# Filling counts in the last stick-breaking head and in the scan, and a five-step block ranking

## The chip, the cores and the metric

The kernel runs on one core of a Trainium2 chip. TensorE (PE in the profile) multiplies matrices, VectorE (DVE), ScalarE (ACT) and GpSimd (POOL) do elementwise work, SyncE (SP) issues the DMA transfers; each engine takes its own instructions in a fixed order and waits on semaphores for the others. The metric is the device time of one execution in microseconds (us), as a median over runs.

## The reference

One decoder layer on x of 1 x 1024 x 1024 in float32. Three mixers read one projection, each is projected back and merged by sigmoid gates, then come an output projection and a gated feed-forward network:

```python
h = rms_norm(x, pre_mix_norm[l])
proj = h @ w_in[l]
z, xbc, dt_raw, sb_qkv, nsa_q, nsa_kv, nsa_gate, merge_gate = jnp.split(proj, split_points(), axis=-1)
y_ssm = ssm_mixer(z, xbc, dt_raw, ...)
y_sb = stick_breaking_attention(sb_qkv)
y_nsa = nsa_attention(nsa_q, nsa_kv, nsa_gate, ...)
gm = jax.nn.sigmoid(merge_gate.astype(jnp.float32)).reshape(bsz, s, 3, D_MODEL)
mixed = (gm[:, :, 0] * (y_ssm @ w_br_ssm[l]) + gm[:, :, 1] * (y_sb @ w_br_sb[l])
         + gm[:, :, 2] * (y_nsa @ w_br_nsa[l])).astype(x.dtype)
x = x + rms_norm(mixed @ w_out[l], post_mix_norm[l])
```

The sparse attention (NSA) ranks 16 blocks of 64 keys for each query by the probabilities of its compressed attention, and keeps eight; some blocks are forced in and later ones are out:

```python
imp_pad = jnp.pad(p_cmp.sum(axis=2), ((0, 0), (0, 0), (0, 0), (1, 0)))
imp = (imp_pad.reshape(bsz, g, NSA_QBLK, nb, ratio).sum(axis=-1)
       + jnp.pad(imp_pad[..., ratio::ratio], ((0, 0), (0, 0), (0, 0), (0, 1))))
imp = jnp.where(valid, jnp.where(forced, BIG, imp), NEG)
_, idx = lax.top_k(imp, n_sel)
```

Stick-breaking attention (four heads) weighs each key by exp(log sigmoid + a sum over the later keys); the SSD scan runs over eight chunks of 128 positions in four groups of heads.

## The kernel before

Every f32 product of the dense projections is made of three: the high part of the weight by the high and the low part of the data, and the low part of the weight by the high part of the data (hi and lo, whi and wlo in the names). All PE instructions are issued at line 235. The program runs in stages: start and the units of the scan's input until about 305 us, preparation and loop of NSA until 745, the stick-breaking heads until about 1080, the scan until about 1275, and then the branch products' rest, output projection and feed-forward network.

Long chains (a score, its exponentials, its products) would leave PE idle, so each stage draws on a pool of independent dense products, a `Fill`: `take(n)` emits n steps of it. A fine step is three products of 128x512. The gates of the merge (tiles named dense, with h_hi and h_lo) fill the attention stages, the branch projections of the three mixers fill the scan (`branches`). What isn't taken in time is emitted at the stage's end by `rest`.

**Stick-breaking.** `attend` (L1470) runs two chains for each head, for the later and the earlier half of the queries: the first with score tiles in ps_s and output in ps_o, the second with ps_t and ps_b. A chain has three steps for each key block: `score` (three products into a bank, then minimum L1411, exponentials L1412 and L1413, copy L1415, maximum L1416), `carry` (one row subtracted L1426, s_hi L1429 on ACT, s_lo L1430 on POOL, and two products of them into the score's bank) and `value` (sum L1441, exponential L1442, w_hi L1446 on ACT, w_lo L1447 on DVE, three products into the output). After each chain step `attend` adds SB_FILL[h] to a remainder and takes its whole part from the pool. In the last head a second pool, `late`, gives two steps more after each chain step past the 24th, bound behind the third last value product; from chain step 30 on the emission order is kept for PE, and ahead of that a scheduler sets it.

**Ranking.** `compressed` (L1065) handles one tile of 128 queries and one key group. From tile 4 on (eight tiles in all) it ranks: sum over the four heads (L1100), sum over the four compressed positions of a block (L1103), on POOL the next block's first position added (L1105), forced and late blocks set by a factor and a summand from `fa` (L1106, L1107), the eight largest (L1109), those replaced by −3e38 (L1111), a comparison that finds which were not replaced (L1112), and times −1e30 into the bf16 tile `aug` (L1113). PE transposes aug, and L1135 copies it into the rows of Q1 that meet the block rows of `c_aug` in the score product, so that blocks not kept get −1e30.

**Scan.** The loop over n steps four generators, one for each group q; a generator stops at "front" (a chunk's preparation), "heads" and "late" (gating, norm and split of a group's result, which make `E.ys[k, h]`, two for each q and half h). `fronts(0)` and `fronts(1)` step the even and odd groups, and `take(SSD_FILL)` with SSD_FILL = 2 fills behind each. The pool's last products read E.ys through k: output unit 0 first six k, unit 1 four, then the last two k of unit 0 (group 3), then the rest. In the names, even groups' rows are `row` and odd groups' `third`.

## Time and profile before

| what | us |
|---|---|
| median of three runs | 2115.36 (2114.43 to 2115.45) |
| profiled execution, its own time | 2113.84 |
| span of the profiled execution | 2111.9 |
| PE busy | 2081.4 |
| DVE, POOL, ACT busy | 1288.7, 1228.7, 1174.8 |

The mean granted clock of TensorE was 0.999. The span is counted from the first to the last instruction. A row of the timeline has the start in the span, the duration, engine, line, operation, the tile written and those read, the shapes, how many were joined (x3), and in brackets the idle time before it with what ended it. Durations of PE products overlap: how long PE needs for one is read from the distance of two starts.

### The profile page before, as it was taken

To read this page: it belongs to the slowest core of one execution; us is meant where nothing else is said; L and a number is where in the kernel's file an instruction comes from. 1 tells how busy PE (TensorE), PEld (TensorE's weight loads), DVE (VectorE), ACT (ScalarE), POOL (GpSimd) and SP (SyncE) were. 2 spreads that over 40 slices of the span, in tenths; PEclk is the share of its full clock that TensorE was granted. 3 is DMA by queue.
4 is the path that set the end of the run, shared out by engine and by line. 5 is a ranking of instruction groups with operands and counts; after the bars stand their busy time and mean duration, and the time that the engine had idled before them with its cause. 6 is when DMAs were issued, how large, how long until landed. Compare 5 with 4: busy or idle time off the path is not lost.

```text
span 2111.9 us, 29407 instructions
## 1 busy us (share of the span) xinstructions
PE 2081.4 (99%) x10069; PEld 1684.8 (80%) x10069; DVE 1288.7 (61%) x2639; ACT 1174.8 (56%) x2124; POOL 1228.7 (58%) x1223
## 2 busy tenths in 40 slices
PE   9999999999999999999999999999999999999998
PEld 7788888877776778888868878887878888888888
DVE  7854453368477046656557774258866666676765
ACT  6554442367757646667765652246554445576634
POOL 1277763158757633334336875557877777766843
PEclk9999999999999999999999999999999999999999
DMA  7333347321220111223274423444223332265532
GB/s 272 95 116 114 110 148 240 110 90 57 78 75 9 45 48 58 63 70 130 91 256 153 147 68 108 141 150 146 86 77 100 100 104 96 100 214 170 160 118 107
DMA packets 129237, 243.92 MB, mean 115 GB/s; under 512 B 14344, under 2 KB 39592, under 8 KB 129088
## 3 DMA queue, kind: packets, MB, share of 16 engines
q1 hardware_dynamic: 127136, 238.94, 34.5%
q10 hardware_dynamic: 1952, 3.11, 0.4%
q8 instruction: 79, 1.29, 0.3%
q14 instruction: 70, 0.57, 0.1%
HBM read 175.83 MB, written 66.17 MB: 115 GB/s over the span
## 4 chain that ended last, share of the span: by engine, by line
PE 87%; DVE 6%; ACT 3%; POOL 2%; issue 1%; DMA 1%; POOLq 0%; ACTq 0%; DVEq 0%; SPq 0%
PE dense L235 57%; PE ps_s L235 10%; PE ps_o L235 8%; PE ps_t L235 7%; PE psn L235 3%; PE ps_b L235 2%; DVE ps_t L1157 0%; DVE x L1922 0%; ACT x L777 0%; DVE u L356 0%; DMA y<-y_d 0%; ACT wT L1189 0%; DMA q_d<-uhi 0%; POOL wlo L308 0%; DVE x L2123 0%
## 5 line engine op out<-in xcount | busy, mean ns | idle before, releaser
L308 POOL TENSOR_TENSOR wlo<-wraw,whi 128x256 fp32r<-128x256 f32 x300 | 239.8, 832 | 171.6 <-ACT whi L303 166.9
L688 POOL TENSOR_TENSOR ulo<-uf,uhi 128x256 fp32r<-128x256 f32 (+1 forms) x174 | 188.8, 1111 | 147.1 <-ACT uhi L712 96.6
L235 PE MATMUL dense<-h_hi,whi 128*128 128x512 f32 x656 | 260.3, 397 | 0.9 <-ACT gate_e L277 0.9
L235 PE MATMUL dense<-h_lo,whi 128*128 128x512 f32 x656 | 256.6, 391 | 0.0
L235 PE MATMUL dense<-h_hi,wlo 128*128 128x512 f32 x656 | 256.4, 391 | 0.0
L1200 POOL TENSOR_TENSOR wT_lo<-wT,wT_hi 128x512 fp32r<-128x512 f32 x132 | 168.4, 1293 | 54.6 <-ACT wT_hi L1199 50.7
L235 PE MATMUL dense<-x,uhi 128*128 128x512 f32 x600 | 190.6, 389 | 0.0
L235 PE MATMUL dense<-hi,wlo 128*128 128x512 f32 x448 | 176.6, 395 | 0.5 <-POOL wlo L308 0.3
L235 PE MATMUL dense<-hi,whi 128*128 128x512 f32 x448 | 174.4, 390 | 0.0
L235 PE MATMUL dense<-lo,whi 128*128 128x512 f32 x448 | 173.2, 391 | 0.0
L235 PEld LDWEIGHTS dense<-h_hi,wlo 128*128 128x128 f32 x656 | 123.2, 188 | 26.6
L235 PEld LDWEIGHTS dense<-h_hi,whi 128*128 128x128 f32 x656 | 123.4, 188 | 24.2 <-ACT gate_e L277 1.1
L235 PEld LDWEIGHTS dense<-h_lo,whi 128*128 128x128 f32 x656 | 123.5, 188 | 23.2
L303 ACT ACTIVATE whi<-wraw 128x1024 fp32r<-128x1024 f32 x76 | 80.3, 1057 | 96.9 <-PE dense L235 87.5
L235 PEld LDWEIGHTS dense<-x,uhi 128*128 128x128 f32 x600 | 112.6, 188 | 23.7
L688 POOL TENSOR_TENSOR wlo<-wraw,whi 128x256 fp32r<-128x256 f32 (+1 forms) x83 | 94.4, 1164 | 60.8 <-ACT whi L703 60.7
L1430 POOL TENSOR_TENSOR s_lo<-sa,s_hi 128x512 fp32r<-128x512 f32 (+2 forms) x48 | 54.2, 1130 | 129.3 <-ACT s_hi L1429 129.3
L356 DVE SCALAR_TENSOR_TENSOR u<-dense,pv,u 128x511 f32<-128x511 f32 (+1 forms) x140 | 103.4, 741 | 33.2 <-ACT u L352 33.0
L1189 ACT ACTIVATE wT<-ps_s 128x512 f32<-128x512 f32 x132 | 78.2, 595 | 47.8 <-PE ps_s L235 42.4
L235 PE MATMUL dense<-x,ulo 128*128 128x512 f32 x264 | 102.9, 390 | 0.0
L235 PEld LDWEIGHTS dense<-hi,wlo 128*128 128x128 f32 x448 | 84.1, 188 | 20.8 <-issue 1.7
L1157 DVE CUSTOM_DVE_ANT_0 ps_t<-ps_t,edges 128x256 f32<-128x256 f32 (+3 forms) x160 | 82.4, 526 | 28.9 <-PE ps_t L235 27.8
(589 smaller groups left out, 5809.0 us busy)
## 6 DMA issues: line engine op xcount, KB each, us to landing
wraw<-in_wfm SPq DMA_DIRECT2D x62, 512.0 KB, 3.9
wraw<-in_wup SPq DMA_DIRECT2D x48, 512.0 KB, 3.6
lo<-m_d SPq DMA_DIRECT2D x58, 256.0 KB, 2.7
g_d<-gate_e SPq DMA_DIRECT2D x48, 256.0 KB, 3.0
s_d<-o SPq DMA_DIRECT2D x48, 256.0 KB, 2.0
m_d<-u SPq DMA_DIRECT2D x44, 256.0 KB, 2.0
row<-g_d SPq DMA_DIRECT2D x36, 256.0 KB, 2.7
row<-s_d SPq DMA_DIRECT2D x32, 256.0 KB, 4.1
```

Of the source, the lines that this page charges most:

```text
L235: return pin(f(*a, **k), in_order)
L303: act(hi, raw, AF.Copy)
L308: eng.tensor_tensor(lo[:, s], raw[:, s], fl(hi[:, s]), op=OP.subtract)
L356: V.scalar_tensor_tensor(o[:, d:], ps[:, :512 - d], taps[d], o[:, d:], op0=OP.mult, op1=OP.add)
L688: eng.tensor_tensor(lo[:, s], x[:, s], fl(hi[:, s]), op=OP.subtract)
L1157: V.tensor_tensor_reduce(pm[:, :w], pm[:, :w], edges[:, 0:w] if edge else edges[:, 640 - w:], 1.0, -3e38, op0=OP.add, op1=OP.max, accum_ou ...
L1189: act(w.rearrange("p h q -> p (h q)"), pz, AF.Exp)
L1200: P.tensor_tensor(lo, wf, fl(hi), op=OP.subtract)
L1430: (P if SB_SLO else V).tensor_tensor(s_lo[:, c0:], a[:, c0:], fl(s_hi[:, c0:]), op=OP.subtract)
```

## The change

It has three parts. In the last stick-breaking head the filling is 1.9 steps behind each chain step instead of 2. In the ranking the sum over heads goes into a tile `sums` that holds for each block four positions and a fifth value, the forced or late summand, which the DMA brings with it; one reduction over six neighbours (four positions, the summand, the next block's first position) gives the ranked value, match_replace writes −1e38 straight into aug, and the copy into Q1 becomes the comparison "greater than −1e37", against block rows of `c_aug` that now hold −1e30. In the scan, four steps in place of two are taken where the first pair of groups has started (n is 1) and behind a "late" stage of groups 2 and 3 in `fronts(1)`.

```diff
-        aug[0, b, b * 64:(b + 1) * 64] = 1.0
+        aug[0, b, b * 64:(b + 1) * 64] = NEG
...
-    fa = np.stack([fac, add], 1).reshape(8, 128, 32).transpose(1, 0, 2).reshape(128, 256)
+    fa = np.zeros((128, 4, 17, 5), f)
+    fa[:, :, :16, 4] = add.reshape(8, 128, 16)[4:].transpose(1, 0, 2)
+    fa = fa.reshape(128, 340)
...
-SB_FILL = (2.2, 2.2, 2.2, 2)
+SB_FILL = (2.2, 2.2, 2.2, 1.9)
...
-    fa = kp.tile([128, 8, 2, 16], F32, name="fa")
-    nc.sync.dma_start(fa.rearrange("p a b c -> p (a b c)"), A["c_fa"])
+    sums = kp.tile([128, 4, 85], F32, name="sums")
+    nc.sync.dma_start(sums.rearrange("p i n -> p (i n)"), A["c_fa"])
...
-            imp = wk.tile([128, 64], F32, name="imp")
-            V.tensor_reduce(imp, p.rearrange("p h n -> p n h"), axis=AX, op=OP.add)
+            s = sums[:, i - 4]
+            blocks = s[:, :80].rearrange("p (b r) -> p b r", r=5)[:, :, 0:4]
+            V.tensor_reduce(blocks, p.rearrange("p h (b r) -> p b r h", r=4), axis=AX, op=OP.add)
             im = wk.tile([128, 16], F32, name="im")
-            iv = imp.rearrange("p (b r) -> p b r", r=4)
-            V.tensor_reduce(im, iv, axis=AX, op=OP.add)
-
-            P.tensor_tensor(im[:, 0:15], im[:, 0:15], iv[:, 1:16, 0], op=OP.add)
-            P.tensor_tensor(im, im, fa[:, i, 0, :], op=OP.mult)
-            P.tensor_tensor(im, im, fa[:, i, 1, :], op=OP.add)
+            six = s[:, 0:81]
+            six = bass.AP(tensor=six.tensor, offset=six.offset, ap=[six.ap[0], [5, 16], [1, 6]])
+            V.tensor_reduce(im, six, axis=AX, op=OP.add)
             top = wk.tile([128, 8], F32, name="top")
             V.max(top, im)
-            left = wk.tile([128, 16], F32, name="left")
-            V.match_replace(left, in_to_replace=top, in_values=im, imm_value=-3e38)
-            V.tensor_tensor(left, left, im, op=OP.is_equal)
-            V.tensor_scalar(aug[:, 64:80], left, NEG, None, op0=OP.mult)
+            V.match_replace(aug[:, 64:80], in_to_replace=top, in_values=im, imm_value=-1e38)
...
-            V.tensor_copy(Q1[64:80, :].rearrange("p (h q) -> p h q", h=4),
-                          p2[64:80, None, :128].to_broadcast([16, 4, 128]))
+            V.tensor_scalar(Q1[64:80, :].rearrange("p (h q) -> p h q", h=4),
+                            p2[64:80, None, :128].to_broadcast([16, 4, 128]), -1e37, None, op0=OP.is_gt)
...
-                    filled = q > 1 or stage[q] == "front"
+                    fills = SSD_FILL * (1 if stage[q] == "front" else (1 + part) * (q > 1))
...
-                    if filled:
-                        take(SSD_FILL)
+                    take(fills)
...
-                take(SSD_FILL if n else SSD_AHEAD)
+                take(SSD_FILL * (1 + (n == 1)) if n else SSD_AHEAD)
```

The numbers move instructions. On PE in the last stick-breaking head, before, between the fourth and the third score from the end of the ps_s chain. ps_s_10434 is a score tile (A), ps_s_10499 the next (B); 18 dense products stand between the ps_t score ahead and B's, of which the last three are shown:

```order
L235 MATMUL dense_10568<-h_hi_82,whi_10561 128x512
L235 MATMUL dense_10568<-h_lo_83,whi_10561 128x512
L235 MATMUL dense_10568<-h_hi_82,wlo_10562 128x512
L235 MATMUL ps_s_10499<-row_9387,row_9390 128x512
L235 MATMUL ps_s_10499<-row_9389,row_9390 128x512
L235 MATMUL ps_s_10499<-row_9387,row_9392 128x512
L235 MATMUL ps_s_10434<-s_hi_10452,rtab_74 128x512
L235 MATMUL ps_s_10434<-s_lo_10453,rtab_74 128x512
L235 MATMUL ps_o_10114<-w_hi_10480,row_9395 128x512
L235 MATMUL ps_o_10114<-w_hi_10480,row_9397 128x512
L235 MATMUL ps_o_10114<-w_lo_10481,row_9395 128x512
```

The same place after the change, where A is ps_s_10357 and B ps_s_10428; the ps_t score's last products are the first two rows:

```order
L236 MATMUL ps_t_10511<-row_9332,row_9334 128x512
L236 MATMUL ps_t_10511<-row_9330,row_9336 128x512
L236 MATMUL dense_10447<-h_hi_82,whi_10375 128x512
L236 MATMUL dense_10447<-h_lo_83,whi_10375 128x512
L236 MATMUL dense_10447<-h_hi_82,wlo_10376 128x512
L236 MATMUL ps_s_10428<-row_9331,row_9334 128x512
L236 MATMUL ps_s_10428<-row_9333,row_9334 128x512
L236 MATMUL ps_s_10428<-row_9331,row_9336 128x512
L236 MATMUL ps_s_10357<-s_hi_10390,rtab_74 128x512
L236 MATMUL ps_s_10357<-s_lo_10391,rtab_74 128x512
L236 MATMUL ps_o_10058<-w_hi_10415,row_9339 128x512
L236 MATMUL ps_o_10058<-w_hi_10415,row_9341 128x512
```

Between the ps_t score and B's stand three dense products now, and the dense products that stood there follow P's value products, the last of which comes behind these rows.

On DVE at the same place, before, from A's minimum on (L1441 with ps_s reads the tile ahead of A, P):

```order
L1411 TENSOR_SCALAR sa<-ps_s 128x512
L1416 TENSOR_TENSOR sa<-ps_s,sa 128x512
L1426 TENSOR_TENSOR sa<-sa,ps_s 1x512
L1441 TENSOR_TENSOR sz<-sz,ps_s 128x512
L1411 TENSOR_SCALAR sa<-ps_t 128x512
```

and after (the lines are four lower):

```order
L1407 TENSOR_SCALAR sa<-ps_s 128x512
L1407 TENSOR_SCALAR sa<-ps_t 128x512
L1412 TENSOR_TENSOR sa<-ps_s,sa 128x512
L1422 TENSOR_TENSOR sa<-sa,ps_s 1x512
L1437 TENSOR_TENSOR sz<-sz,ps_s 128x512
L1407 TENSOR_SCALAR sa<-ps_s 128x512
```

The ps_t score's minimum has moved ahead of A's maximum, and so ahead of the reading of P's bank.

On PE in the scan, before, behind the transposes (ps_t<-ident,row) of group 3's first half, from the last transpose of the next chunk's preparation to the products of unit 0 that read group 3's rows (the last two rows):

```order
L235 MATMUL ps_t<-third 128x128
L235 MATMUL ps_s<-row,whi 128x512 x2
L235 MATMUL ps_s<-row,wlo 128x512
L235 MATMUL ps_s<-row,whi 128x512 x2
L235 MATMUL ps_s<-row,wlo 128x512
L235 MATMUL ps_s<-third,whi 128x512 x2
L235 MATMUL ps_s<-third,wlo 128x512
L235 MATMUL ps_s<-third,whi 128x512 x2
L235 MATMUL ps_s<-third,wlo 128x512
L235 MATMUL ps_s<-third,whi 128x512 x2
L235 MATMUL ps_s<-third,wlo 128x512
```

After, from those transposes of group 3's first half on:

```order
L236 MATMUL ps_t<-ident,row 128x128 x4
L236 LDWEIGHTS sel
L236 MATMUL dense<-row,sel 128x512
L236 MATMUL ps_t<-ident,third 128x128 x3
L236 MATMUL ps_t<-third 128x128
L236 MATMUL ps_s<-third,whi 128x512 x2
L236 MATMUL ps_s<-third,wlo 128x512
L236 MATMUL ps_s<-third,whi 128x512 x2
L236 MATMUL ps_s<-third,wlo 128x512
```

The 12 products of the units' earlier rows that stood between are gone from here (they stand ahead of the transposes), and the products that read group 3's rows are the next but the preparation.

## The prediction

> **What bounds the kernel.** I read the busy times and the chain on the page first, then TensorE's list of waits, then the timeline at each place where the change moves something.

> ```profile
> PE 2081.4 (99%) x10069; PEld 1684.8 (80%) x10069; DVE 1288.7 (61%) x2639; ACT 1174.8 (56%) x2124; POOL 1228.7 (58%) x1223
> PEclk9999999999999999999999999999999999999999
> PE 87%; DVE 6%; ACT 3%; POOL 2%; issue 1%; DMA 1%; POOLq 0%; ACTq 0%; DVEq 0%; SPq 0%
> ```

> TensorE is busy for 2081.4 of 2111.9 us, and the chain that ended last is 87% its own. The change removes no matrix product. So nothing is won but TensorE's idle time, 2111.9 − 2081.4 = 30.5 us in the whole program, and nothing is lost but new idle time. VectorE and GpSimd are busy for about 60%; work taken from them counts only where TensorE waits for it. Each term below is therefore a wait of TensorE that goes, or one that comes.

> **Unit of filling.** Neighbouring dense products start 0.23 us apart (1067.46 and 1067.69 in the fence after next; the listed 0.39 overlaps the next product). A step of filling is three, 0.69 us.

> **Part 1, the last stick-breaking head (1.9 steps in place of 2).** The lower count delays filling, and the printed order shows where it goes: the fourth score tile from the end of the ps_s chain (call the last four A, B, C, D) has about as many dense products behind it as before, 150 against 151. Behind B stand 144 against 120, behind C 119 against 84, behind D 84 against 72. So filling that stood between A and B now stands behind B.

> What goes: behind D two places were too thin.

> ```profile
> 1056.95 0.40 PE L235 MATMUL dense<-h_hi,wlo 128*128 128x512 f32 x1
> 1058.37 0.96 PE L235 MATMUL ps_s<-row 128*128 128x512 f32 x3 [1.01 <-DVE sz L1441]
> ```
> ```profile
> 1067.46 0.39 PE L235 MATMUL dense<-h_lo,whi 128*128 128x512 f32 x1
> 1067.69 0.39 PE L235 MATMUL dense<-h_hi,wlo 128*128 128x512 f32 x1
> 1068.67 0.73 PE L235 MATMUL ps_o<-w_hi,row 128*128 128x512 f32 x2 [0.59 <-ACT w_hi L1446]
> 1069.82 0.50 PE L235 MATMUL ps_o<-w_lo,row 128*128 128x512 f32 x1 [0.42 <-DVE w_lo L1447]
> ```

> Start to start, less the products themselves, these cost 1.42 − 0.23 = 1.19, 0.98 − 0.23 = 0.75 and 1.15 − 0.46 = 0.69: **2.6 us**. After, D has 35 instead of 12 dense products ahead of it, and the pair of w_hi 12 instead of 6 (1.4 us more). I take all 2.6 as gone.

> What comes: look at what hung between A and the values of the tile ahead of it (call that tile P).

> ```profile
> 1033.30 0.28 PE L235 MATMUL ps_b<-w_lo,row 128*128 128x256 f32 x1
> 1033.57 0.69 DVE L1411 TENSOR_SCALAR sa<-ps_s 128x512 f32<-128x512 f32 x1 [1.96 <-PE ps_s L235]
> ...
> 1037.02 2.83 POOL L308 TENSOR_TENSOR wlo<-wraw,whi 128x256 fp32r<-128x256 f32 x4 [6.70 <-ACT whi L303]
> ...
> 1037.94 0.62 ACT L1429 ACTIVATE s_hi<-sa 128x512 fp32r<-128x512 f32 x1
> ...
> 1039.81 1.34 POOL L1430 TENSOR_TENSOR s_lo<-sa,s_hi 128x512 fp32r<-128x512 f32 x1
> ...
> 1040.51 0.62 ACT L1446 ACTIVATE w_hi<-sz 128x512 fp32r<-128x512 f32 x1
> ...
> 1041.15 0.69 DVE L1447 TENSOR_TENSOR w_lo<-sz,w_hi 128x512 fp32r<-128x512 f32 x1 [1.16 <-ACT w_hi L1446]
> ...
> 1043.61 0.40 PE L235 MATMUL ps_o<-w_lo,row 128*128 128x512 f32 x1
> 1043.84 0.40 PE L235 MATMUL dense<-h_hi,whi 128*128 128x512 f32 x1
> ```

> A's products are done at 1033.3. Its s_lo exists only at 39.81 + 1.34 = 1041.15, because GpSimd first splits a weight (2.83 us); P's w_lo exists at 41.15 + 0.69 = 1041.84. Before, 31 dense products filled that time, and A's s_hi and s_lo products and P's value products followed at once, until 1043.84. After, only 6 dense products stand there: behind the ps_t score come three, then B's score, A's s_hi and s_lo, and P's three value products, with no dense product between them. TensorE reaches B's score at about 1036.5 (the 1033.3 plus 14 products, the narrow ones shorter). B's bank is that of P, which L1441 frees; in the new order on VectorE L1441 stands behind the ps_t score's L1411. That gives 1038.6. A's s_lo keeps the same two operations ahead of it on GpSimd: about 1041.1. P's w_hi now follows A's s_hi and the ps_t score's exponentials on ScalarE: about 1042.2, w_lo 43.1. So the value products end near 1043.4, 0.44 us earlier than before, with 24 dense products (24 × 0.23 = 5.5 us) still to run. Five us of new idle time: **+5.0**. Bounds: 0 below (if those dense products could run ahead after all; they cannot in this order unless the chain is faster), 5.5 above. The nearest rows are those quoted, so I take 5.0. Queued behind the waiting products are the 24 dense ones and, for those, ScalarE's gates (L277), which nobody needs soon. Part 1: 5.0 − 2.6 = **+2.4 us**.

> Nothing waited for TensorE's filling between 960 and this place, so the slightly thinner filling there costs nothing; its cover is the rest of the filling, and a whole product less at each step would cost 0.23.

> **Part 2, the ranking (eight tiles).** It takes L1105 to L1107 from GpSimd and L1112 and L1113 from VectorE; L1103 reads 96 elements instead of 64.

> ```profile
> L1105 POOL TENSOR_TENSOR im<-im,imp x8: 218/227/235, 448.9 to 652.1; 128x15 f32<-128x15 f32 x8
> ...
> L1109 DVE MAX8 top<-im x8: 172/173/178, 450.3 to 655.2; 128x8 f32<-128x16 f32 x8
>   PEld ps_t L235: 0.5, 1
> L1112 DVE TENSOR_TENSOR left<-left,im x8: 165/354/1207, 450.9 to 656.7; 128x16 f32<-128x16 f32 x8
>   PEld ps_t L235: 0.2, 1
> L1113 DVE TENSOR_SCALAR aug<-left x8: 156/175/690, 451.4 to 657.4; 128x16 bf16<-128x16 f32 x8
> ```

> By the medians that is 8 × (0.35 + 0.18) = 4.2 us off VectorE and 8 × 3 × 0.22 = 5.4 off GpSimd. L1135 becomes a comparison of the same 16x512 tile from PSUM, L1111 writes bf16: both at the old price. The wider L1103 and the strided output of L1100 are not in the trace: 0 at least, and at most another L1109-sized 0.17 each, 2.8 us for eight, which would still leave VectorE lighter. How much reaches TensorE?

> ```profile
> 420.00:700.00 280.00, 272.15 (x1358) 198.44 (x1357) 188.13 (x649) 191.85 (x360) 193.34 (x213) 1.00 0.22 63
> ```
> ```profile
> L235 PE MATMUL ps_t<-K,Q 96*128 96x384 f32 (+3 forms) x176 | 61.8, 364 | 3.4 <-DVE mx L1157 1.9 <-DVE mx L1160 0.7 <-DVE Q L1174 0.5
> ```

> In the loop TensorE idles 7.85 us in all, of which 3.4 us behind VectorE's maxima. Only 0.5 + 0.2 us hang directly on ranking instructions (the two indented rows, the waiters of the row above each). VectorE is busy for 188 of 280 us, so it makes up a delay soon after. **−0.7 us**; bounds −3.4 and, if the strided forms are dear, +0.7.

> **Part 3, the scan.** The order shows eight steps, 24 products, pulled forward from the run behind the scan, which waits for nothing. They come at four places.

> At the beginning two steps more ahead of a wait:

> ```profile
> 1098.63 0.61 PE L235 MATMUL ps_b<-dec,xd 128*64 128x128 f32 x8
> 1099.94 0.66 PE L235 MATMUL ps_o<-dec,xd 128*64 128x128 f32 x8 [0.71 <-ACT ce L1545]
> ```

> Less 0.49 for the eight products this costs 0.8; 1.38 us of filling cover it: **−0.8**. Near the end:

> ```profile
> 1265.28 0.40 PE L235 MATMUL dense<-row,wlo 128*128 128x512 f32 x1
> 1266.99 0.66 PE L235 MATMUL ps_t<-ident,row 128*128 128x128 f32 x4 [1.32 <-ACT row L1611]
> ...
> 1272.31 0.40 PE L235 MATMUL dense<-third,wlo 128*128 128x512 f32 x1
> 1273.10 0.66 PE L235 MATMUL ps_t<-ident,row 128*128 128x128 f32 x4 [0.39 <-ACT row L1611]
> ```

> 1.71 − 0.23 = 1.5 and 0.79 − 0.23 = 0.56, each now behind two steps more (1.38): **−1.4** and **−0.55**. The fourth place costs:

> ```profile
> 1252.40 0.60 PE L235 MATMUL ps_t<-ident,row 128*128 128x128 f32 x4
> ...
> 1253.52 0.71 PE L235 MATMUL ps_s<-row,whi 128*128 128x512 f32 x2
> ...
> 1256.37 1.00 PE L235 MATMUL ps_s<-third,whi 128*128 128x512 f32 x2
> ...
> 1258.66 0.50 PE L235 MATMUL ps_s<-third,whi 128*128 128x512 f32 x1 [0.83 <-DVE third L1623]
> ```

> The transposes at 1252.40 begin the chain that makes the output rows of group 3; the fill products from 1256.37 read those rows, and already wait for them. Between stood 12 products (1253.52 to 1256.37). The pulled-forward steps use those up ahead of the transposes, so the reading products come straight after them: TensorE arrives 2.8 us earlier and the rows come no sooner, save about 0.4 where VectorE starts the chain earlier. **+2.4**, between 0 (the rows as early as wanted) and 2.8. Queued behind the waiting product are the last fill steps of this unit and group 3's ps_o products, for which VectorE waits to begin the next head; they come later by the same amount, which is inside the sum.

> Scan: −0.8 − 1.4 − 0.55 + 2.4 = **−0.35**.

> **Sum.** 2.4 − 0.7 − 0.35 = +1.35 us on the profiled execution's 2113.84 (span 2111.9): 2115.2. The median of the runs is 1.5 above that execution: 2115.36 + 1.35 = **2116.7**, no change that can be told (0.2%, 4.2 us, is about what a measurement of this kernel can tell).

> **Rivals.** *The filling is not locked out between A and P's values* (a faster chain, by a shorter weight split on GpSimd): part 1 gives −2.6, the sum −3.65, **2111.7**. For it: nothing waits there before. Against it: 1041.15, which no part of the change makes earlier. *That, and the wait at 1258 does not grow*: part 3 −2.75, sum −6.05, **2109.3**; against it is the consuming order. *The ranking is worth all of VectorE's 3.4*: **2114.0**; against it, VectorE's slack. *The covers fail*, since what is waited for is issued behind the added filling too, and only the two new waits stay, with part 2 off the path: 5.0 − 2.6 + 2.4 = +4.8, **2120.2**. That is also what is left if the change does not do what it says. *The slower side by one mechanism: TensorE's clock.* The longest wait named in the waits is 1.3:

> ```profile
> PE ps_t L235 <- ACT row L1611: 1.7, 2, 1.3
> ```

> Stands of 5.0 (in pieces) and some 3.7 us at 1258 are outside what this trace shows at full clock. If the granted clock, 9 in every slice of the page, fell to half afterwards for as long as each stand, half of 8.7 us would be lost, 4.35: **2121**. It decides as soon as a stand of over 3 us lowers the clock at all.

> [...] The stands come in pieces with products between, and no row here shows such a drop, so I give it little.

> **Numbers.** Forecast 0.46; filling not locked out 0.17; that and no growth 0.12; ranking worth more 0.08; covers fail 0.10; clock 0.07. The second lies astride the bound of faster (2111.1), half each way. Faster 0.12 + 0.08 + 0.03 (tails) = 0.23; slower 0.10 + 0.07 + 0.01 = 0.18; same 0.59. The range runs from 2110.5 to 2120.5 and leaves out the third and the last.

> **What would show it.** Right: in TensorE's waits of the changed kernel, waits for s_hi, s_lo and w_hi of about 5 us together near 1036 to 1043, none at 1057 and 1068; a wait on L1623's counterpart of 3 to 4 us in all near 1255; none of 1.3 on row L1611's. Wrong: dense products between B's score and A's s_lo, or the PEclk row below 9 there. If the loop from 420 to 700 idles under 5 us, part 2 was sized too small.

## The result and the profile after

| | us |
|---|---|
| kernel before, median of 6 runs beside the changed one | 2114.89 (2113.94 to 2116.05) |
| changed kernel, median of 6 runs | 2126.44 (2124.03 to 2128.31) |
| ratio after to before, 95% interval | 1.0054 [1.0043, 1.0066] |
| span of the profiled execution, before and after | 2111.9 and 2125.3 |
| mean granted clock, before and after | 0.999 and 0.995 |

The changed kernel is slower by 11.5 us, outside the range and on the side that had a chance of 0.18. The page of the changed kernel: first the busy times, then the granted clock, then the chain by engine.

```profile
PE 2089.4 (98%) x10061; PEld 1689.7 (80%) x10069; DVE 1286.0 (61%) x2623; ACT 1174.4 (55%) x2124; POOL 1220.9 (57%) x1199
...
PEclk9999999999999999999999999999999999999999
...
PE 86%; DVE 6%; ACT 3%; POOL 2%; issue 1%; DMA 1%; SPq 0%; POOLq 0%; ACTq 0%; DVEq 0%
```

The number of products is the same (the 8 rows fewer are records that are missing: PEld has 10069 in both), and yet TensorE is busy 8.0 us longer. That goes with a slower clock: 0.995 was granted, and 0.999 before. The PEclk row doesn't show it: a slice is 53 us wide, and 9 stands for 90% or more. It is no matter of one execution: all six of the changed kernel were granted 0.995 or 0.996. The idle time grew from 30.5 to 2125.3 − 2089.4 = 35.9 us, by 5.4. So the loss is 5.4 us of waits and 8.0 us of slower products. TensorE's list of waits, longest single ones (line, what is waited for: sum, times, longest):

```profile
PE dense L236 <- DMA row<-ac_d: 2.6, 1, 2.6
PE ps_s L236 <- DVE sz L1437: 2.1, 1, 2.1
...
PE ps_s L236 <- ACT third L1618: 1.7, 1, 1.7
...
PE ps_s L236 <- ACT y L1665: 1.6, 2, 1.1
```

The second and third were forecast (at B's score and at group 3's rows). The first and the last were not: both go back to loads that SyncE issues. In the kernel before, no single wait in TensorE's list was longer than 1.3 us.

**Where the 13.4 us of span went.** I took the starts of the same products in both traces and compared the stretches between them. Where a stretch holds six products more than before, their 1.38 us (6 x 0.23) are taken off, and 2.76 us are added where it holds twelve fewer. Stretches in which a run's program is that of before also differ by up to 0.8 us from profile to profile, and by more where a single wait comes or goes.

| stretch | before | after | difference | forecast |
|---|---|---|---|---|
| start to A's score | 1032.38 | 1032.16 | −0.2 | −0.7 |
| A's score to the scan's first selection product | 48.96 | 53.69 | +4.7 | +2.4 |
| on to the first state update (the y products) | 10.43 | 12.12 | +1.7 | 0 |
| on to the second (the doubled begin) | 8.76 | 9.20, six more | −0.9 | −0.8 |
| second to eighth | 61.52 | 61.64 | +0.1 | 0 |
| eighth to ninth (the load row<-ac_d) | 11.78 | 16.10 | +4.3 | 0 |
| ninth to sixteenth | 75.27 | 75.85 | +0.6 | 0 |
| on to the first ps_t<-ones (group 3's rows) | 12.75 | 18.96, six more | +4.8 | +2.4 |
| on to the end of the span (the waits on row L1611) | 850.05 | 845.58, twelve fewer | −1.7 | −1.95 |

The last score tiles of the stick-breaking head, in TensorE's timeline of the changed kernel (start, duration, operation, in brackets the idle time before it and what ended it):

```profile
1035.83 0.40 PE L236 MATMUL dense<-h_hi,wlo 128*128 128x512 f32 x1
1038.34 0.96 PE L236 MATMUL ps_s<-row 128*128 128x512 f32 x3 [2.11 <-DVE sz L1437]
1039.67 0.50 PE L236 MATMUL ps_s<-s_hi,rtab 128*128 128x512 f32 x1 [0.36 <-ACT s_hi L1425]
1041.24 0.79 PE L236 MATMUL ps_s<-s_lo,rtab 128*128 128x512 f32 x1 [1.07 <-POOL s_lo L1426]
1042.26 1.22 PE L236 MATMUL ps_o<-w_hi,row 128*128 128x512 f32 x2 [0.23 <-ACT w_hi L1442]
1043.34 0.79 PE L236 MATMUL ps_o<-w_lo,row 128*128 128x512 f32 x1
1043.93 0.63 PE L236 MATMUL dense<-h_hi,whi 128*128 128x512 f32 x1
1044.36 0.63 PE L236 MATMUL dense<-h_lo,whi 128*128 128x512 f32 x1
...
1047.68 0.39 PE L236 MATMUL dense<-h_hi,whi 128*128 128x512 f32 x1
1047.91 0.39 PE L236 MATMUL dense<-h_lo,whi 128*128 128x512 f32 x1
```

B's score starts at 1038.34 (worked out: 1038.6), A's s_lo product at 1041.24 (1041.1), P's values at 1042.26 (1042.2). But look at the dense products behind: they start 0.43 us apart, from 1043.93 on, and 0.23 apart again from 1047.68 on. Nothing is named in brackets, so they don't wait; they run at about half speed. At group 3's rows the same picture:

```profile
1268.48 0.51 PE L236 MATMUL ps_s<-third,whi 128*128 128x512 f32 x1 [1.69 <-ACT third L1618]
1269.87 0.80 PE L236 MATMUL ps_s<-third,whi 128*128 128x512 f32 x1 [0.88 <-DVE third L1619]
1270.46 0.63 PE L236 MATMUL ps_s<-third,wlo 128*128 128x512 f32 x1
```

Apart from the first 7 and the last 8 us, the granted clock changes in the changed kernel at 1040.74, 1047.56, 1177.27, 1180.68, 1269.43 and 1276.26, three times down and up. Stretches of 3.41 us cut at these times (duration, then busy time and instructions of PE, PEld, DVE, ACT, POOL, then PEclk, DMA share, GB/s):

```profile
1037.33:1040.74 3.41, 1.46 (x4) 0.67 (x4) 2.19 (x4) 3.41 (x8) 3.41 (x5) 1.00 0.01 2
1040.74:1044.15 3.41, 2.68 (x5) 1.50 (x6) 2.96 (x7) 3.40 (x7) 1.27 (x2) 0.50 0.63 231
1044.15:1047.56 3.41, 3.41 (x9) 2.64 (x9) 3.11 (x5) 1.36 (x3) 0.60 (x2) 0.50 0.00 0
1047.56:1050.97 3.41, 3.41 (x16) 2.79 (x16) 0.69 (x1) 1.06 (x2) 1.15 (x1) 1.00 0.00 0
1173.86:1177.27 3.41, 1.21 (x8) 1.14 (x9) 0.86 (x4) 1.86 (x7) 2.38 (x2) 1.00 0.91 338
1177.27:1180.68 3.41, 3.41 (x9) 2.64 (x8) 2.67 (x6) 2.09 (x6) 0.00 (x0) 0.50 0.31 94
...
1266.02:1269.43 3.41, 1.28 (x8) 0.71 (x5) 2.58 (x4) 3.15 (x9) 1.27 (x1) 1.00 0.00 0
1269.43:1272.85 3.42, 2.83 (x6) 1.83 (x7) 2.18 (x4) 0.56 (x2) 0.00 (x0) 0.50 0.00 0
1272.85:1276.26 3.41, 3.41 (x10) 2.64 (x9) 0.69 (x1) 0.70 (x1) 2.63 (x4) 0.50 0.00 0
```

Read the first row of each of the three groups: TensorE was busy for 1.46, 1.21 and 1.28 of 3.41 us, still at full clock. Then come one or two stretches at 0.50, and after a wholly busy one the clock is back. The clock's changes all lie whole multiples of 3.41 us apart (1047.56 to 1177.27 is 38 of them, 1180.68 to 1269.43 is 26, and from 1276.26 to its fall at 2119.35, behind the last product, it is 247), so in this trace they lie on one grid through the program, and at all three places the clock falls at the end of a stretch in which TensorE was busy for less than half. The half clock's price, from the pitch of the products behind (0.43 less 0.23 each): about 2.3 us at the score, 1.7 at row<-ac_d (half of 3.41) and 2.4 at group 3's rows, 6.4 in all. The stretches at 0.50 hold 15.7 us of TensorE's busy time (2.68 + 3.41 + 3.41 + 2.83 + 3.41), and half of that is 7.9, so the half clock accounts for the 8.0 us; what is over the 6.4 I put down to slow products inside the stands, where TensorE would have waited anyway.

The load for which the longest wait stands. The profile's view of SyncE's own queue, the changed kernel:

```profile
1168.04 0.38 SPq L1674 DMA_DIRECT2D y<-yl_d  x1
1168.51 0.38 SPq L1674 DMA_DIRECT2D y<-y_d  x1
1168.99 0.38 SPq L1674 DMA_DIRECT2D y<-yl_d  x1
1169.46 0.35 SPq L1514 DMA_DIRECT2D row<-ac_d  x1
```

and the kernel before:

```profile
1160.71 0.59 SPq L1678 DMA_DIRECT2D y<-yl_d  x1
1161.39 1.23 SPq L1518 DMA_DIRECT2D row<-ac_d  x1
1163.24 0.33 SPq L1678 DMA_DIRECT2D y<-y_d  x1
```

Before, row<-ac_d was issued at 1161.39, ahead of the last two pairs of y loads. The six products pulled forward at the begin bring these pairs forward in the program, ahead of row<-ac_d, and y loads have to wait until a fill product has freed a y tile (between 1145 and 1180 SyncE waits 6.1 us for such products ahead of them). So row<-ac_d is issued at 1169.46 only. Of the 8 us that this is later on the clock, 6.8 are the delay of the whole program by then; counted from the eighth state update (1162.05 and 1168.81) the issue is 1.3 us later. The way is longer too: the selection product that needs the row began 5.2 us after the issue before, without a wait, and begins 6.6 us after it now, with eight y loads issued just ahead. TensorE stands 2.57 us for it, until 1176.06. The y products at the beginning of the scan (+1.7) are late in a like way: the first of their loads is issued 4.0 us ahead of the first selection product and not 4.4, and the first split of a y row begins 5.3 us after that issue and not 4.5. Ahead of these loads (first one at 1081.88) stand two weight loads at 1080.27 and 1081.33, where before there was one at 1076.49; that they are the reason is not shown.

### The profile page after: what moved, and what is told of

Same layout as the page of the kernel before. It is cut to its first block, busy times and chain, and to the rows that moved or that the text cites. A ratio compares the mean times of both kernels' runs of the same rounds, so it can differ in the third digit from the quotient of the medians.

```text
span 2125.3 us, 29355 instructions
## 1 busy us (share of the span) xinstructions
PE 2089.4 (98%) x10061; PEld 1689.7 (80%) x10069; DVE 1286.0 (61%) x2623; ACT 1174.4 (55%) x2124; POOL 1220.9 (57%) x1199
## 4 chain that ended last, share of the span: by engine, by line
PE 86%; DVE 6%; ACT 3%; POOL 2%; issue 1%; DMA 1%; SPq 0%; POOLq 0%; ACTq 0%; DVEq 0%
PE dense L236 56%; PE ps_s L236 10%; PE ps_o L236 7%; PE ps_t L236 7%; PE psn L236 3%; PE ps_b L236 3%; DVE x L1917 0%; DVE ps_t L1153 0%; ACT wT L1185 0%; ACT x L778 0%; DVE u L357 0%; DVE x L2118 0%; DVE osq L1878 0%; DMA row<-ac_d 0%; DMA q_d<-uhi 0%
```

## The experiments

Each is compared with the kernel before, on the same chip; ratios with 95% intervals. A profile is one execution, up to 2 us away from the median of its kernel's runs, so a place is read from the profiles and the time from the medians. First the four parts alone (before: 2115.37 us, median of 28 runs).

**The stick-breaking count alone.**

```diff
-SB_FILL = (2.2, 2.2, 2.2, 2)
+SB_FILL = (2.2, 2.2, 2.2, 1.9)
```

> The kernel before with SB_FILL 1.9 in the last head alone. Theory W+C (waits, and half clock behind each long one): the order on TensorE in the head is that of the changed kernel, so A to the first product of the scan costs +4.7 us and the first loads of the scan 1.7 more, about +6.3 us, 2121; granted clock about 0.97 between 960 and 1085. Theory W (waits alone, as forecast): +2.4 us, clock 1.00 throughout. Rival (the ranking or the scan made the loss): within 1 us of before.

Measured: 2121.97 us, 1.0030 [1.0018, 1.0041]; span +6.2 us. A's score to the first selection product is 3.9 us longer than before, and the y products behind it 2.3 us, of which a part is again half clock (from 1090.26 to 1093.67). The stretches of its clock grid at the score:

```profile
1035.65:1039.06 3.41, 1.30 (x6) 0.70 (x5) 2.65 (x4) 2.91 (x5) 1.78 (x3) 1.00 0.01 2
1039.06:1042.48 3.42, 2.24 (x5) 0.68 (x3) 2.71 (x6) 3.42 (x8) 2.26 (x3) 0.50 0.37 115
1042.48:1045.89 3.41, 3.41 (x8) 2.34 (x9) 3.01 (x5) 2.31 (x5) 1.28 (x1) 0.50 0.30 115
1045.89:1049.30 3.41, 3.41 (x17) 2.79 (x16) 1.98 (x4) 1.90 (x3) 1.30 (x1) 1.00 0.00 0
```

What follows: this part alone gives more than half of the loss, and the waits of the sum (2.4 us) are less than half of what it costs.

**The ranking alone** (its hunks of the diff).

> The ranking alone. Both theories: -0.5 us (the loop from 430 to 745 lost 24.3 us beyond the usual pitch in the changed kernel, 24.8 before), so no change that can be told, at 2114.4. Rival (the ranking is worth all of VectorE's waits): -3.4 us. VectorE's order behind the loop is that of before, so nothing else should move.

Measured: 2114.2 us, 0.9996 [0.9987, 1.0005]. TensorE comes to the stick-breaking head about 0.9 us earlier, but not all of that is the ranking: the run called "The late steps only where the waits are" below, with the ranking of before, comes there 0.8 us earlier too. What the ranking's loop itself gives is seen by following the same products through it: from 400 to 735 us they gain 0.6 us on before here, 0.5 in the changed kernel and 0.4 to 0.5 in the other four profiles with the new ranking; without it four profiles stay between −0.1 and +0.1, and two lose 1.1 and 2.1 at a wait near 636. The gain is as small as forecast, and can't be told from none in the time.

**The doubled begin alone.**

```diff
-                take(SSD_FILL if n else SSD_AHEAD)
+                take(SSD_FILL * (1 + (n == 1)) if n else SSD_AHEAD)
```

> Two steps more at the scan's beginning alone. Theory Q (the third load of decay rows, row<-ac_d, now stands behind all eight pairs of y loads on SyncE instead of six, and the last two pairs wait for buffers): -0.9 us at 1099, then a wait of 2 to 3 us for row<-ac_d near 1170 and a lower clock behind it, in all about +3.4 us, 2118.3. Rival (the wait for row<-ac_d came from the last head's delayed loads): -0.9 us in all and no such wait.

Measured: 2117.93 us, 1.0012 [1.0003, 1.0021]. Its waits and its clock grid:

```profile
PE dense L235 <- DMA row<-ac_d: 2.0, 1, 2.0
```
```profile
1168.12:1171.53 3.41, 1.37 (x10) 0.93 (x9) 1.50 (x5) 2.39 (x7) 3.24 (x3) 1.00 0.98 369
1171.53:1174.95 3.42, 3.42 (x10) 2.64 (x9) 2.90 (x6) 2.41 (x7) 0.00 (x0) 0.50 0.32 105
```

The begin alone brings the wait for row<-ac_d, and a half clock behind it. (The profiled execution, 2119.83 us, is one of the slower of its eleven.)

**The late steps alone** (the hunk in `fronts`).

> The fuller late stages of the scan alone. Theory W+C: the place behind group 3's transposes costs +4.85 us with half clock near 1260 to 1268, the two waits on row L1611 save 2.0, so about +2.8 us, 2117.7. Theory W: +2.4 - 2.0 = +0.4 us, clock 1.00.

Measured: 2116.07 us, 1.0000 [0.9991, 1.0008]. Both waits on row L1611 are gone, and group 3's rows cost 1.4 us more than before, in pieces, in this profile at full clock:

```profile
1257.17 0.50 PE L235 MATMUL ps_s<-third,whi 128*128 128x512 f32 x1 [0.29 <-ACT third L1622]
1258.58 0.50 PE L235 MATMUL ps_s<-third,whi 128*128 128x512 f32 x1 [0.91 <-DVE third L1623]
...
1260.38 0.51 PE L235 MATMUL ps_s<-third,whi 128*128 128x512 f32 x1 [0.83 <-DVE third L1623]
```

Here only six of the twelve products between the transposes and the reading ones are used up ahead; the begin uses the other six. Each alone costs 1.4 us there, both together 4.8, 2.0 more than the sum. The four parts alone sum to 6.6 − 1.2 + 2.6 + 0.7 = 8.7 us, and the change costs 11.5; the 2.0 are of the size of what is missing, but with intervals of about 2 us on each part the difference of 2.8 is not clear of noise. The profiled execution (2114.12 us) is one of the five of eleven that were granted 0.999; these took 2114.8 us on average, the four with 0.998 took 2116.1 and the two with 0.997 took 2117.7. So the lower clock comes in some executions of this kernel and not in others.

The second four (before: 2114.72 us, median of 27 runs).

**The late steps only where the waits are.**

```diff
+                    fills = SSD_FILL * (1 if stage[q] == "front" else (1 + (part and n > 16)) * (q > 1))
```

> The doubled late filling alone, and only from the step (n > 16) at which the waits on row L1611 stand; the products ahead of group 3's transposes stay as in the kernel before. Theory (the late filling covers the two waits, and its whole loss comes from the products that it uses up ahead of the reading ones): the two waits of 1.5 and 0.56 us go, the stand at the third L1623 stays at 1.3 us in all, time 2.0 us below before (ratio about 0.9990). Rival (the filling is only moved, and the run behind the scan then waits for what it reads): the waits go, the same 2 us come back between 1275 and 1400, ratio 1.000.

Measured: 2112.82 us, 0.9988 [0.9979, 0.9997]. Nothing is left of the waits on row L1611, group 3's rows cost what they cost before, and the filling isn't missed later. This term of the sum (−1.95) was right.

**Work in the stand at group 3's rows.** The changed kernel and 12 products with a weight of zeros, which add nothing to the open bank:

```diff
+                for _ in range(0 if j else 12):
+                    mm(outs[0][0], zr, E.ys[0, 0][0], start=False, stop=False)
```

> The whole change, and 12 products with a weight of zeros more (2.8 us of TensorE's time at full clock), added to the open bank ahead of the products that read group 3's rows, where the changed kernel stands for 3.2 us. They add nothing to the result. Theory (a stand halves the granted clock for some us behind it): TensorE is now busy where it stood, the clock stays at 1.00 from 1266 to 1280, and the kernel with more work is 2 to 2.5 us faster than the changed kernel: ratio to before about 1.0044 in place of 1.0054. Rival (the clock falls there for another reason, or the lost 4.85 us are waits throughout): 1.0054 as the changed kernel, and a clock of 0.5 to 0.6 from 1270 to 1276 again.

Measured: 2123.78 us, 1.0039 [1.0027, 1.0052]. The timeline, and a window that reaches over the place:

```profile
1263.81 3.01 PE L236 MATMUL ps_s<-row,zr 128*128 128x512 f32 x12
...
1268.95 0.50 PE L236 MATMUL ps_s<-third,whi 128*128 128x512 f32 x1 [0.83 <-DVE third L1619]
```
```profile
1266.00:1278.00 12.00, 11.07 (x62) 8.37 (x61) 8.06 (x11) 4.64 (x9) 8.06 (x9) 1.00 0.14 45
```

The clock stays at 1.00 (the changed kernel: 0.72 over the same window), and from the sixteenth state update to the first ps_t<-ones it takes 2.0 us less with 2.8 us more work. So here the half clock came from the stand, not from the work at the place. The span as a whole is 3.0 us shorter than the changed kernel's: in this profile the wait for row<-ac_d was 1.31 us and not 2.57, and the clock did not fall behind it, 2.8 us less there; near 1870, 1.7 us are lost again, 1.0 of them at waits for snap (2.1 us in all and not 1.1). So the stand at one and the same place was 2.57 us with half clock behind it in one profile, and 1.31 us without in another.

**The begin, with row<-ac_d issued early.**

```diff
-            if n == at:
-                if q > 1:
-                    acs[q] = ac_t(q)
+            if q > 1 and n == at - 4:
+                acs[q] = ac_t(q)
+            if n == at:
```

> The doubled begin alone, with the loads row<-ac_d of units 2 and 3 issued four steps earlier, so that on SyncE they stand ahead of the y loads that wait for buffers. Against the run with the begin alone (ratio 1.0012, wait of 2.0 us for row<-ac_d, clock 0.79 behind it). Theory (the load is late because it is queued behind loads that wait): no wait for row<-ac_d, clock 1.00 from 1168 to 1180, 2.5 to 3.5 us less than that run: ratio 0.9998 to 1.0002 (begin -0.9, the stand at group 3's rows +1.4). Rival (the load itself is slow, or the wait only moves to the y loads, now one place later): a wait of over 1 us stays between 1160 and 1185, ratio 1.001 or more.

Measured: 2115.55 us, 1.0006 [0.9997, 1.0015]. The window over the place is full, at full clock:

```profile
1160.00:1180.00 20.00, 20.00 (x145) 16.00 (x144) 15.15 (x34) 12.81 (x35) 15.55 (x14) 1.00 0.59 200
```

Issued early enough, the load costs nothing, so it was late by its place in SyncE's queue; how much of that is the later issue and how much the longer way behind the y loads, this run doesn't part. What is left of the begin's loss is the 1.4 us at group 3's rows.

**The paying parts together**: ranking, begin with the early loads and with its two steps given back at n = 9, late steps from n > 16, and 2 steps in the stick-breaking head.

```diff
-                take(SSD_FILL if n else SSD_AHEAD)
+                take(SSD_FILL * {0: 3, 1: 2, 9: 0}.get(n, 1))
```

> The parts that should pay, together: the ranking, the doubled begin with the early row<-ac_d loads and with its two steps given back where unit 3 begins (n = 9), and the late filling only from n > 16; the stick-breaking head as before. Theory, by the single parts: ranking -0.5, begin -0.9, the waits on row L1611 -2.05, nothing at group 3's rows: 3.5 us below before, ratio 0.9983. Rival (taking the filling away where unit 3 begins opens a new wait there, or the parts take each other's cover as in the changed kernel): 0.9990 to 1.000.

Measured: 2112.24 us, 0.9986 [0.9977, 0.9995]. The rival was right in part: the six products had covered a wait where they were taken away.

```profile
1182.64 0.52 PE L236 MATMUL ps_t<-ident,row 128*128 128x128 f32 x3 [1.54 <-DVE row L1616]
```

The last three (before: 2114.55 us, median of 15 runs).

**Given back elsewhere.**

```diff
-            take(SSD_FILL)
+            take(SSD_FILL * (n != 13))
```

> As the run before with all paying parts, but the two steps of the doubled begin are given back in the middle of the scan (n = 13, the fill steps behind the heads of unit 2 alone) and no longer where unit 3 begins, where they opened a wait of 1.7 us for row L1616. Theory (those six products covered that wait; elsewhere the chain has slack): no wait over 1 us between 1100 and 1250, 1.0 to 1.5 us less than that run, 3.5 us below before, ratio 0.9983. Rival (every fill step of the scan covers something): a wait of 1 to 1.7 us turns up between 1200 and 1235, ratio 0.9986 again.

Measured: 2112.44 us, 0.9989 [0.9980, 0.9998]. There is no such wait between 1100 and 1250, as expected, but a new one of 0.82 us at 1276.94, which the eviction of a unit (L1734) ends, some 0.8 us more are lost near 1870, and the gain is no larger. Neither theory named that place. Three kernels with the late steps at the right place are thus some 2 us faster than before; they can't be told apart.

**Work in the stand at B's score.** The stick-breaking part alone, and 18 products with a weight of zeros ahead of B's score:

```diff
+                    for _ in range({(carry, 4): 12, (value, 3): 6}.get((f, m), 0) if (h, c) == (3, 1) else 0):
+                        mm(po, zr, q_hi[c], start=False, stop=False, skip_group_check=True)
```

> The stick-breaking part alone (ratio 1.0030, +6.3 us on the profiled span), and 18 products with a weight of zeros more (4.1 us of TensorE's time at full clock), added to the open output bank ahead of B's score, where TensorE stands for 2.1 us and then in pieces. They add nothing to the result. Theory (the stand halves the clock): the clock in 1036 to 1048 is 0.97 or more in place of 0.76 and 0.68, and the first dense product behind P's values starts at 1043 to 1044 and the next twelve take 0.23 us each in place of 0.43, so that although 4.1 us of work were added, the first selection product of the scan starts 1 to 3 us earlier than with the part alone; the order behind is a little other than there, so the end may differ by one us more. Rival (the clock falls with the change of work at this place, stand or no stand): 0.7 again in both stretches, and the scan begins as late or later than there.

Measured: 2122.61 us, 1.0039 [1.0026, 1.0051].

```profile
1037.52 4.30 PE L235 MATMUL ps_o<-row,zr 128*128 128x512 f32 x18
...
1042.81 0.85 PE L235 MATMUL ps_s<-row 128*128 128x512 f32 x3
...
1044.67 0.39 PE L235 MATMUL dense<-h_hi,whi 128*128 128x512 f32 x1
1044.90 0.39 PE L235 MATMUL dense<-h_lo,whi 128*128 128x512 f32 x1
```
```profile
1036.00:1042.00 6.00, 6.00 (x28) 4.97 (x28) 3.27 (x5) 3.06 (x6) 1.29 (x1) 1.00 0.00 0
1042.00:1048.00 6.00, 6.00 (x28) 4.90 (x27) 2.57 (x4) 5.69 (x11) 2.83 (x4) 1.00 0.07 5
```

At the place the clock theory holds: 1.00 in both windows (0.76 and 0.68 with the part alone), a pitch of 0.23. From A's score to the first dense product behind P's values it takes 9.9 us instead of 11.8, with 4.1 us more work. The other half of the expectation failed: the scan begins 2.3 us later than with the part alone, not 1 to 3 us earlier. Two things are in that. A's score itself starts 2.5 us later here, of which 2.1 are lost near 636, in the ranking's loop, at a wait of 1.3 us with a stretch of half clock behind it (637.97 to 641.38); the run with the begin alone has the same wait there, without the added products. Counted from A's score, the scan begins 0.2 us earlier, with 4.1 us more work. And the added products changed the order behind, so that D's score now stands for a long time:

```profile
1063.02 0.96 PE L235 MATMUL ps_s<-row 128*128 128x512 f32 x3 [2.20 <-DVE sz L1443]
```
```profile
1061.22:1064.63 3.41, 1.61 (x7) 1.35 (x8) 2.15 (x4) 1.89 (x3) 1.30 (x1) 1.00 0.00 0
1064.63:1068.05 3.42, 3.42 (x18) 2.87 (x17) 1.44 (x3) 1.72 (x3) 0.00 (x0) 1.00 0.00 0
```

This stand of 2.20 us is longer than that at B's score (2.11), and the clock behind it stays at 1.00. A border of the grid (1061.22) lies inside the stand, so that the stretch holds 1.80 us of idle time, and seven products. So the length of a stand alone did not decide here.

**The whole change with row<-ac_d early.**

> The whole change with the row<-ac_d loads of units 2 and 3 issued four steps earlier, ahead of the y loads on SyncE. Theory (the stand of 2.57 us for row<-ac_d and the half clock behind it are 4.3 us of the loss): no wait for row<-ac_d, clock 1.00 in 1160 to 1182, and 4 us less than the changed kernel: ratio 1.0035. Rival (the time comes back at the products that read group 3's rows, where the stand grows by as much): 1.005 or more.

Measured: 2123.49 us, 1.0038 [1.0026, 1.0051], against 1.0054. The wait is gone and the stretch between the eighth and ninth update takes 4.3 us less; the y products took 1.4 us longer in this profile than in the changed kernel's (here a stretch at half clock, from 1091.76 on, lies in them), and group 3's rows cost nearly as much (18.42 − 1.38 − 12.75 = 4.3 us over before, not 4.8). The begin's wait and what follows from it is worth about 3 us of the 11.5 (2.6 by the medians, 3.4 by the spans; the two intervals overlap, so the place itself, with its 4.3 us, is the better witness).

## Why the prediction was wrong

- **The first step held in part**: the time is bound by TensorE's own chain, and waits that go or come count. But "nothing is lost but new idle time" failed: it took a product's time as given. The trace of before shows a pitch of 0.23 us, at a clock of 1.00 all the way from 5.1 to 2107.7 us; 8.0 us of the loss are products at half clock.
- **Part 1 (+2.4)**: the waits were right, place by place, within 0.3 us up to P's w_hi, and those at 1057 and 1068 went as worked out. The stretch lost 4.7. (TensorE's named waits there add up to 3.8 us and not 5.0; products at half clock fill part of the stand.) The 2.3 us more are the half clock: shown by the part alone and by the zero products. The clock was among the rivals, with a chance of 0.07. The sign named for it, a PEclk row below 9, could not show so short a drop. The condition given there, "a stand of over 3 us", is wrong, and so is the price, half as long as the stand. No single wait that had half clock behind it reached 3 us: the longest was 2.57 us. In these profiles 1.95 us of idle time or more within one stretch of the grid had half clock behind it every time, and so had 1.27 once.
- **What part 1 left out**: the y loads at the scan's begin, +1.7 in the changed kernel and +2.3, partly half clock, in the part alone. The sum counted no DMA of this part. That two weight loads stand ahead of them is read from SyncE's queue; no run moved these loads alone.
- **Part 2 (−0.7)**: about right: −0.5 within the ranking's loop in the changed kernel's profile, −0.6 in the part's own. The −0.2 of the table and the −0.9 of the part hold besides what was lost or won ahead of the loop. The wider reduction took 0.245 us in place of 0.212, inside the bounds.
- **Part 3, begin (−0.8)**: the cover gave −0.9. But the step pulled loads forward as well as products, and I followed only the products: +4.3 at row<-ac_d, of which 2.6 are the wait and 1.7 the clock. This is the step that was missed outright, a term put at nothing without a reason; moving the load took it away.
- **Part 3, group 3's rows (+2.4)**: the mechanism was right. The named waits are 2.6 us, where 3 to 4 were expected; the term came to 4.8, the rest being the half clock, which the zero products took away.
- **Part 3, row L1611 (−1.95)**: right, −2.0, and alone worth about 2 us in the whole time.

Added up, with the price of the half clock taken off: the waits and covers that were in the sum gave −0.2 + 2.4 − 0.9 + 0.1 + 2.4 − 1.7 = 2.1 us, against 1.35 forecast. The three half clocks (6.4), the wait for row<-ac_d (2.6) and the y loads (1.7), together 10.7, were not in it. With the 0.6 between the ninth and sixteenth update that is the 13.4 us of span. The 0.6 seem to belong to the doubled begin: the profiles that have it, and give nothing back, show 0.6 to 1.0 there, of the five without it four show 0.0 (the ranking alone 1.8, at two single waits). Which wait makes them is open.

## What to carry to other kernels

A stand of TensorE cost more than its own length here (4.3 us for a wait of 2.57): before adding one, add up all idle time within the 3.41 us of the grid seen here, pieces too, and reckon with half a clock behind it; in these runs it came sometimes from 1.25 us on and every time from 1.95, and lasted 3.41 or 6.82 us. Where a step of filling is moved, follow its loads through SyncE's queue: y loads that had to wait for a free tile held back the load behind them here, though that was wanted earlier. A change in several parts that draw on one pool is tested part by part and together, since two parts can each take half of the same cover.

## What the runs showed of the hardware

Idle time alone did not decide here. In 13 of these 28 stretches only products of 128x512 start: the eight with four or five of them (idle 1.27 to 2.11 us) were followed by half clock, the five with six or seven (1.26 to 1.80 us) were not. And near the program's end, where the products have 1 to 128 columns, the clock of the changed kernel fell at 2119.35 behind a stretch with 1.13 us. What decides between 1.25 and 1.8 us no run here tests.

The kernel before has at most 1.32 us in a stretch in its profile (1264.62 to 1268.03), and the next stretch is at 1.00; that lies among the 1.25 to 1.8 us that had half clock behind them in 5 of 21 cases. Its executions differ: of the 70 beside the experiments 58 were granted 0.999 and took 2114.9 us on average, 11 were granted 0.998 and took 2116.4, and one, with 0.997, took 2117.2. One stretch of 3.41 us at half clock costs half of that, 1.7 us, 0.0008 of the span, by estimate.

In two runs work whose result is nothing kept the clock up: with products of zero weights in the stand, the clock was 1.00 (without them 0.72 at group 3's rows, 0.76 and 0.68 at the score), and the products behind it kept their pace of 0.23 us.
